# Placing the Sigmoids of the merge gates one product later, and reordering the first ScalarE work of the attention

## The chip, the cores and the metric

The kernel runs on one NeuronCore of a Trainium2 chip. The metric is the time of one execution on the device in microseconds (us), as the median of several runs. One execution is also recorded by the hardware profiler. Engines: TensorE (PE; its weight loads are shown as PEld), VectorE (DVE), ScalarE (ACT), GpSimd (POOL), and SyncE (SP), whose queue issues nearly all DMAs.

## The reference

One decoder layer over x of 2048 rows and 1024 columns (SEQ, D_MODEL), all in float32. A conditioning vector c gives shift, scale and gate. Two token mixers work side by side, a sliding-window attention with sinks and a causal pool over windows of 2, 4, 8 and 16 rows; each has a SiLU gate and an output projection, and two sigmoid gates merge them:

```
mod = silu(c) @ w_ada + b_ada;  shift, scale, gate = split(mod, 3)
u = x * (1 + scale) + shift
q, k, v, a_gate, p_in, p_gate, m_a, m_p = split(u @ w_in)     # widths 1024,128,128,1024,1024,1024,1024,1024
a = (sliding_window_sink_attention(q, k, v, sinks, bias, mask) * silu(a_gate)) @ w_attn_proj
p = ((multiscale_causal_pool(p_in) through w_pool_mix) * pool_scale * silu(p_gate)) @ w_pool_proj
y = (sigmoid(m_a) * a + sigmoid(m_p) * p) @ w_out * (1 + gate)
x = layer_norm(alpha * x + y)
```

There are 16 query heads of 64 columns on 2 key/value heads, and a window and block of 128 rows.

## The kernel before, in words

**Products.** Every large matrix product is done with operands split in two fp32r parts, high and low (three matmuls for one), and with a Strassen-like scheme of seven products on a 2 x 2 blocking instead of eight. One "product" is 12 matmuls of 128 x 128 weights against 512 columns (`product`, L317). The data side of a product is a *set*: B11, T1, T2, B21, T3, B22, T4. Each set lies in SBUF in two halves (blocks 0 and 1, and blocks 2 and 3 of the inner dimension), each half with a high and a low part: ACT casts it to the high part, DVE subtracts to get the low part. The weight side is a `Quad`: four blocks of weights (`W` and `A22`), whose sums POOL makes (`sum1` L269, `mid` L273 and L274, `late` L278), and whose parts ACT (cast, L306 or L313) and DVE (low, L132) write into `w_set` tiles, of which there are four.

**The ring.** Outside the attention, quads go in groups of two. For a group, `front` (L331) makes the opening products with B11 and T1, two for each quad. Then `back` (L341) makes T2 and B21 for the first quad and for the second, T3 and B22 for the first and for the second, and the two T4. That is 14 products for a group with the opening of the next. After each product stands a `tick()`: it first runs the hooks of its position in the group, then everything in the list `due` that `defer(ticks, f)` (L454) put off to this tick. Four accumulators pass to `consume` as they are ready: the first behind B21, then T3, B22 and T4 (the T3 result goes through `p <- lg, p`, L390).

**The order of the queues.** `pe`, `act`, `dve`, `pool` and `sp` are wrappers (`Ordered`, L51). Whatever goes through them is pinned behind the last instruction traced before it on the same engine; their line in the profile is always L57. What is written as `nc.scalar...`, `nc.vector...` is not pinned: the compiler's scheduler places it, by the time at which it expects the operands to be there. Each engine then has one fixed queue.

**Stages.** The head and the first ring compute gates, keys, values and queries of the first half of the rows (1024 rows each); `attention` (L774) follows for the first half; a second ring and `attention` for the second half. Then comes the output part, rings of its own: the merge gates left over, then attention projection, pool projection (first half), attention projection, pool projection (second half), each of two groups, and last the product with w_out with the layer norm. `planned` (L530) hangs the set work of each stage at fixed positions: B11, T1, T2 and B21 and the first half of T3 in the last group of the stage before, the second half of T3, then B22 and T4 by halves at positions 0 to 4 of the stage's first group.

**The merge gates.** Their raw values (`ma_d`, `mp_d`) were stored to DRAM by earlier stages. `gates_ahead` (L599) loads them: at the beginning of `back` two tiles for each quad of the group, and two ticks later the other two, by `sp.dma_start`, and each has its Sigmoid (`nc.scalar.activation`, L607). `consume` of an attention projection (L614) multiplies the result by the gate on DVE (L618); that of a pool projection (L625) multiplies (L627), adds to the attention's part (L629) and stores y.

**The attention.** `attention` writes out by hand, all through the pinned wrappers, the work of 64 blocks of queries (scores, softmax, transposes, values) and, between them, the products of the remaining gates, queries and pool inputs as fill; the list `seq` holds the order of the fill's products, and `split(i)` makes the weights of number i (cast on ACT, low part on POOL or DVE), three products ahead. Numbers 0, 1 and 2 are T2, B21 and T3 of the first quad. At the start (L987 to L997) stand: the load of the last keys and values of the first half (second attention only), the first bias tile, `warm` (an Exp on one column, which makes the table of Exp be loaded), `seed(0)` (ACT copies the first opening accumulator), the copy of the second one to `p5`, and the three first `split`. The two opening products before the attention are made by `front`, with SiLUs of the last gates (L587) about them.

Of the kernel before, what the change touches and what calls it, by code (L numbers as in the profile page):

```python
# [14 lines left out]
AF = mybir.ActivationFunctionType  # L15
# [45 lines left out]
def kernel(  # L61
# [22 lines left out]
    nc = tc.nc  # L84
# [46 lines left out]
    def low(engine, dst, src, hi):  # L131
        engine.tensor_tensor(dst, src, as32(hi), ALU.subtract)  # L132
# [9 lines left out]
    def bank(tag="mm"):  # L142
        return ps.tile([P, CH], F32, tag=tag, bufs={"mm": 4, "lg": 2, "pt": 1, "pv": 1}[tag], name=tag)
# [310 lines left out]
    def defer(ticks, f):  # L454
        due.append((now[0] + ticks, len(due), f))
# [143 lines left out]
    def gates_ahead(name, s, m, raw):  # L599
        g = {}  # L600

        def ahead(ph, turn):
            for mi, t in (((0, 0), (1, 1)), ((0, 1), (1, 0)))[turn]:
                x = g[mi, t] = ph.c("g")
                sp.dma_start(x, gates_d[name][s, m + mi, t])
                if raw:
                    nc.scalar.activation(x, x, AF.Sigmoid)  # L607

        return g, ahead

# [137 lines left out]
    def load_kv(s):  # L748
        if s:
            sp.dma_start(as32(kk[:, :, 0:P]), k_end_d)  # L750
            sp.dma_start(as32(vv[:, 0]), v_end_d)
# [22 lines left out]
    def attention(ph, s, fills, post, opened):  # L774
# [10 lines left out]
        def bias_tile(j):  # L785
            bt = tp.tile([P, 2, 2 * P], F32, tag="bt", bufs=2, name="bt")
            e_src = e_rep[:, 2 * j : 2 * j + 2, :]
            sp.dma_start(bt, bass.AP(e_src.tensor, e_src.offset + P - 1, [[HEADS * ET - 1, P], [ET, 2], [1, 2 * P]]))
            return bt
# [92 lines left out]
        splits = {}  # L882
# [9 lines left out]
        def split(i):  # L892
            x, name = seq[i]
            q = quads[x]
            if name == "B11" and x > 1:
                q.sum1(pool)
            w = ph.split()
            hi, lo = made[i] = w[:, 0:CH], w[:, CH:]
            act.copy(hi, q.block(name))
            low(dve if name == "T1" or (x, name) in on_dve else pool, lo, q.block(name), hi)  # L900
            if name == "T1":
                q.mid(pool)
            elif name == "B21":
                q.late(pool)
# [18 lines left out]
        def seed(x):  # L923
            st[x][2] = bank()
            act.copy(st[x][2], st[x][0])
# [21 lines left out]
        def filling():  # L947
            for i, (x, name) in enumerate(seq):
                begun(i)
                w = made.pop(i)  # L950
                acc = st[x][{"B11": 0, "B21": 0, "T1": 1, "B22": 1}.get(name, 2)]
                for k in range(4):
                    product(acc, w, name, name in ("B11", "T1"), k, k + 1)
                    yield
                ended(i)
# [30 lines left out]
        U = 2 * NB  # L986
        load_kv(s)  # L987
        bts = {0: bias_tile(0)}
        act.activation(warm, mhalf, AF.Exp)
        seed(0)  # L990
        p5 = st[0][3] = tp.tile([P, CH], F32, tag="p5", bufs=2, name="p5")
        act.copy(p5, st[0][1])
        for i in range(-3, 0):
            for j in splits.get(i, ()):
                split(j)
        fill = filling()
        lgs, exps, Ls, pvs, outs, ags = {}, {}, {}, {}, {}, {}  # L997
        total, done = 4 * len(seq), 0
# [1 line left out]
        for n in range(N + 3):  # L1000
            now_n[0] = n
            j, t, b = n // U, n // NB % 2, n % NB
# [547 lines left out]
    with Pools("a0") as ph:  # L1550
        opened = attention(ph, 0, plans[0][1], plans[0][2], opened)
# [4 lines left out]
    with Pools("a1") as ph:  # L1556
        opened = attention(ph, 1, plans[1][1], plans[1][2], opened)
# [3 lines left out]
    with Pools("mix", spare=4, p=2, c=8) as ph:  # L1561
# [10 lines left out]
        for n, (raw, i) in enumerate((raw, i) for raw in (ain_d[1], pin_d[1], wo_d) for i in range(4)):  # L1572
            for offset, f in sums_to(ph, raw, i, load_raw(raw, i)):
                at = int(2 + 8 * n + offset)
                i, gi = every[at // 14]
# [78 lines left out]
```

## Time and profile before

| | us |
|---|---|
| median of 3 runs | 1693.23 |
| lowest, highest | 1687.39, 1694.29 |
| the profiled execution | 1693.3 |
| span of its trace, first to last instruction | 1691.5 |
| PE busy | 1648.7 |
| DVE busy | 1193.7 |
| ACT busy | 1030.0 |
| POOL busy | 988.5 |

The span is what the trace covers; the rest of the execution's time lies around it. Times in rows are microseconds from the first instruction. A row of the timeline has start, duration, engine, line, operation, what it writes and reads, shapes, how many instructions of the kind follow one another, and in brackets how long the engine stood idle before it and what released it. A row of windows has the stretch, its length, PE's busy time with the number of instructions, the granted clock of PE (1.00 is full speed), the DMA share and GB/s.

### The profile page before, as it was taken

The page shows a single profiled execution, that of the slowest core. Times are in us where ns is not written, and L with a number is a line of the kernel's source. Part 1 is how long each engine was busy: PE and PEld are TensorE (multiplying, and loading weights), DVE is VectorE, ACT ScalarE, POOL GpSimd, SP SyncE. Part 2 cuts the span into 40 slices and gives each one's busy share as a digit, 9 for nine tenths or more (in the row PEclk, how much of TensorE's full clock was granted, in tenths as well). Part 3 has the DMA queues.
Part 4 walks back from the last instruction along what each step waited for, and adds up shares of the span by engine and source line. Part 5 has one row for each costly group of instructions (what it writes and reads, how often), then busy time and mean ns, then how long its engine had stood idle before and what let it go on. Part 6 is the DMA issues. An engine that isn't in the chain of part 4 may idle for free.

```text
span 1691.5 us, 24675 instructions
## 1 busy us (share of the span) xinstructions
PE 1648.7 (97%) x8058; PEld 1384.4 (82%) x8058; DVE 1193.7 (71%) x2132; ACT 1030.0 (61%) x2150; POOL 988.5 (58%) x734
## 2 busy tenths in 40 slices
PE   7999999999999999999999999999999999999997
PEld 6788888888888888888788888888878777887886
DVE  6856545676857657357567677676669897989877
ACT  4755457878778755335578777876646445644452
POOL 3343437586857828762476867496567576533442
PEclk9999999999999999999999999999999999999999
DMA  9688843343432478766533344234979797888443
GB/s 359 219 279 307 197 161 102 101 132 108 149 107 99 135 248 308 267 231 211 190 114 99 114 130 156 81 114 135 336 247 363 262 360 259 318 283 271 150 150 112
DMA packets 188849, 336.79 MB, mean 199 GB/s; under 512 B 18336, under 2 KB 44080, under 8 KB 188720
## 3 DMA queue, kind: packets, MB, share of 16 engines
q1 hardware_dynamic: 185600, 330.96, 57.3%
q10 hardware_dynamic: 3088, 4.23, 1.0%
q8 instruction: 64, 1.05, 0.2%
q14 instruction: 65, 0.53, 0.1%
q0 software_dynamic: 32, 0.02, 0.0%
HBM read 227.96 MB, written 110.33 MB: 200 GB/s over the span
## 4 chain that ended last, share of the span: by engine, by line
PE 74%; DVE 8%; DMA 7%; ACT 4%; issue 3%; POOL 3%; SPq 1%; POOLq 0%; DVEq 0%; ACTq 0%
PE mm L57 48%; PE lg L57 19%; PE pv L57 4%; PE pt L57 4%; DVE w_set L132 1%; DMA ain_T<-spare 1%; ACT L L57 1%; DMA g<-ma_d 1%; DMA g<-mp_d 1%; DVE w_set L57 1%; DVE set_T L57 1%; POOL W L269 1%; DMA spare<-pin_B 1%; DVE L L57 1%; ACT w_set L57 1%
## 5 line engine op out<-in xcount | busy, mean ns | idle before, releaser
L57 PE MATMUL mm<-set_B,w_set 128*128 128x512 f32 x2664 | 655.8, 393 | 2.2 <-DVE w_set L132 1.2
L57 PEld LDWEIGHTS mm<-set_B,w_set 128*128 128x128 f32 x2664 | 497.1, 189 | 107.0 <-DVE w_set L132 2.4
L57 PE MATMUL mm<-set_T,w_set 128*128 128x512 f32 x1824 | 455.5, 396 | 5.9 <-DVE mm L57 3.9
L57 PE MATMUL lg<-set_T,w_set 128*128 128x512 f32 x1704 | 412.6, 392 | 10.5 <-DVE p L390 4.4
L57 PEld LDWEIGHTS mm<-set_T,w_set 128*128 128x128 f32 x1824 | 336.7, 189 | 76.2 <-DVE mm L57 6.5
L57 PEld LDWEIGHTS lg<-set_T,w_set 128*128 128x128 f32 x1704 | 319.9, 189 | 81.8 <-ACT w_set L306 5.2
L132 DVE TENSOR_TENSOR w_set<-W,w_set 128x1024 fp32r<-128x1024 f32 x137 | 197.8, 1445 | 142.3 <-ACT w_set L306 129.3
L306 ACT CAST w_set<-W 128x1024 fp32r<-128x1024 f32 x137 | 143.8, 1050 | 212.7 <-PE mm L57 124.3
L57 POOL TENSOR_TENSOR w_set<-W,w_set 128x512 fp32r<-128x512 f32 x120 | 157.3, 1318 | 116.9 <-ACT w_set L57 112.0
L269 POOL TENSOR_TENSOR W<-W,A 128x512 f32<-128x512 f32 x46 | 74.1, 1610 | 232.5 <-DMA A<-in_win_dram 63.5
L57 DVE TENSOR_TENSOR o<-pv,o 64x128 f32<-64x128 f32 x256 | 72.1, 282 | 133.7 <-ACT o L57 127.3
L57 POOL TENSOR_TENSOR spare<-spare 128x512 f32<-128x512 f32 x68 | 124.0, 1826 | 31.5 <-DMA spare<-pin_B 12.2
L57 POOL TENSOR_TENSOR W<-W 128x512 f32<-128x512 f32 x82 | 108.3, 1336 | 53.2 <-DVE sm L57 31.0
L57 ACT ACTIVATE L<-L,nm 128x257 f32<-128x257 f32 (+1 forms) x256 | 127.2, 499 | 9.3 <-DVE nm L57 3.7
L278 POOL TENSOR_TENSOR W<-W 128x512 f32<-128x512 f32 x46 | 72.8, 1583 | 95.9 <-DVE w_set L132 83.5
L57 DVE CUSTOM_DVE_ANT_0 L<-lg,bt,nsink 128x256 f32<-128x256 f32 (+1 forms) x256 | 111.7, 473 | 21.3 <-PE lg L57 11.9
L57 ACT CAST w_set<-W 128x512 fp32r<-128x512 f32 (+1 forms) x165 | 101.4, 628 | 20.9 <-POOL W L57 14.9
L273 POOL TENSOR_TENSOR W<-W 128x512 f32<-128x512 f32 x44 | 72.7, 1656 | 66.3 <-DVE w_set L132 57.2
L57 ACT COPY o<-pv 64x256 f32<-64x256 f32 x128 | 47.4, 370 | 75.9 <-PE pv L57 74.7
L57 DVE TENSOR_TENSOR ptl<-pt,pth 128x512 fp32r<-128x512 f32 (+1 forms) x128 | 85.7, 669 | 1.3 <-ACT pth L57 1.0
L274 POOL TENSOR_TENSOR W<-W 128x512 f32<-128x512 f32 x44 | 71.6, 1628 | 21.9 <-DMA W<-in_win_dram 18.9
L57 ACT ACTIVATE L<-L,sm 128x256 f32<-128x256 f32 (+1 forms) x128 | 64.3, 502 | 31.7 <-DVE sm L57 31.4
(230 smaller groups left out, 2398.2 us busy)
## 6 DMA issues: line engine op xcount, KB each, us to landing
W<-in_win_dram SPq DMA_DIRECT2D x42, 512.0 KB, 5.4
W<-in_win_dram SPq DMA_DIRECT2D x42, 256.0 KB, 3.7
A<-in_win_dram SPq DMA_DIRECT2D x42, 256.0 KB, 4.9
ag_d<-sig SPq DMA_DIRECT2D x32, 256.0 KB, 5.7
pg_d<-sig SPq DMA_DIRECT2D x32, 256.0 KB, 4.4
pg<-pg_d SPq DMA_DIRECT2D x32, 256.0 KB, 3.2
pin_B<-fin SPq DMA_DIRECT2D x32, 256.0 KB, 2.0
ag<-ag_d SPq DMA_DIRECT2D x32, 256.0 KB, 2.9
```

The costliest lines, as they stand in the source:

```text
L57: return lambda *args, **kw: self.tc.keep_in_program_order(op(*args, **kw))
L132: engine.tensor_tensor(dst, src, as32(hi), ALU.subtract)
L269: e.tensor_tensor(self.w[:, 1, :], self.w[:, 2, :], self.a22, ALU.add)
L273: e.tensor_tensor(x[:, 1, :], x[:, 1, :], x[:, 0, :], ALU.subtract)
L274: e.tensor_tensor(x[:, 2, :], x[:, 0, :], x[:, 2, :], ALU.subtract)
L278: e.tensor_tensor(x[:, 3, :], x[:, 3, :], x[:, 1, :], ALU.subtract)
L306: a.copy(by_two(hi), raw)
```

## The change

In `gates_ahead`, each Sigmoid is no longer given out right behind its load but through `defer(1, ...)`: it is traced at the next tick, one product later. At the start of `attention`, the weights of T2 and B21 (`split` of numbers 0 and 1) are made first, then the seed copy, then the warm-up of the Exp table, then the copy to `p5`, and then the weights of T3.

```
@@ gates_ahead
                 sp.dma_start(x, gates_d[name][s, m + mi, t])
                 if raw:
-                    nc.scalar.activation(x, x, AF.Sigmoid)
+                    defer(1, lambda x=x: nc.scalar.activation(x, x, AF.Sigmoid))
@@ attention
         bts = {0: bias_tile(0)}
+        for i in (-3, -2):
+            for j in splits.get(i, ()):
+                split(j)
+        seed(0)
         act.activation(warm, mhalf, AF.Exp)
-        seed(0)
         p5 = st[0][3] = tp.tile([P, CH], F32, tag="p5", bufs=2, name="p5")
         act.copy(p5, st[0][1])
-        for i in range(-3, 0):
-            for j in splits.get(i, ()):
-                split(j)
+        for j in splits.get(-1, ()):
+            split(j)
```

## The prediction

> **What bounds the kernel now.** I read the page, then TensorE's (PE's) busy time in windows, then the order of instructions around each window in which PE lost time. The page first:
>
> ```profile
> span 1691.5 us, 24675 instructions
> ## 1 busy us (share of the span) xinstructions
> PE 1648.7 (97%) x8058; PEld 1384.4 (82%) x8058; DVE 1193.7 (71%) x2132; ACT 1030.0 (61%) x2150; POOL 988.5 (58%) x734
> ```
>
> PE is busy for 97%, so only its idle time (42.8 us, much of it at the head, which the change does not touch) and its slow time (a lowered clock counts as busy) can be won. The windows of the places that the change does touch: the starts of the two attentions, then four first groups and one second group of the stages with the merge gates, 14 products each, cut at starts of products.
>
> ```profile
> 256.10:264.20 8.10, 6.68 (x23) 0.79 0.14 52
> 829.50:836.00 6.50, 5.21 (x23) 1.00 0.42 131
> ```
>
> ```profile
> 1218.20:1263.30 45.10, 41.05 (x168) 0.92 0.78 261
> 1263.30:1301.40 38.10, 38.10 (x169) 1.00 1.03 384
> 1301.40:1343.50 42.10, 39.86 (x169) 0.96 0.70 237
> 1383.80:1423.70 39.90, 39.04 (x169) 1.00 0.70 254
> 1461.90:1500.40 38.50, 38.50 (x169) 1.00 0.60 200
> ```
>
> Columns: length, PE busy (instructions), granted clock, DMA share, GB/s. The group at 1263, a second one, shows no wait: 38.1 us, so 2.72 for a product (12 matmuls). Call the first groups A1 to A4 (starts at 1218, 1301, 1384, 1462; attention, pool, attention, pool): they lose 7.0, 4.0, 1.8 and 0.4 us. Each attention window holds 18 matmuls of fill (18 x 2.72 / 12 = 4.1 us) and one block's scores (0.3 to 0.5 us), so 4.5 us: the first attention loses 3.6, the second 2.0. All of this together is 18.8 us, 1.1% of the time.
>
> **The change part by part. The attention.** Its instructions stand in an order fixed by the program, and each engine works off its queue in order. ScalarE (ACT) around the first start, in two stretches; then PE's waits and GpSimd (POOL):
>
> ```profile
> 247.79 1.28 ACT L57 ACT_TABLE_LOAD   x1
> 249.09 0.20 ACT L57 ACTIVATE warm<-mhalf 128x1 f32<-128x1 f32 x1
> 249.31 1.28 ACT L587 ACT_TABLE_LOAD   x1
> 250.60 1.09 ACT L587 ACTIVATE sig<-lg 128x512 f32<-128x512 f32 x2
> ```
>
> ```profile
> 256.36 0.59 ACT L57 COPY p<-mm 128x512 f32<-128x512 f32 x1 [2.10 <-PE mm L57]
> 256.84 1.66 ACT L57 CAST w_set<-W 128x512 fp32r<-128x512 f32 x3
> 258.40 0.19 ACT L57 COPY L<-nsink 128x2 f32<-128x2 f32 x1
> 258.61 1.28 ACT L57 ACT_TABLE_LOAD   x1
> 259.90 0.40 ACT L57 ACTIVATE L<-L,nm 128x129 f32<-128x129 f32 x1
> ```
>
> ```profile
> 257.51 0.73 PE L57 MATMUL mm<-set_T,w_set 128*128 128x512 f32 x2 [0.80 <-ACT w_set L57]
> 258.87 0.50 PE L57 MATMUL mm<-set_T,w_set 128*128 128x512 f32 x1 [0.62 <-POOL w_set L57]
> ```
>
> ```profile
> 249.77 1.48 POOL L273 TENSOR_TENSOR W<-W 128x512 f32<-128x512 f32 x1
> 257.54 1.28 POOL L57 TENSOR_TENSOR w_set<-W,w_set 128x512 fp32r<-128x512 f32 x1 [6.29 <-ACT w_set L57]
> ```
>
> The warm-up loads Exp's table at 247.79, the last two SiLUs of the gates (L587) load their own over it, and Exp loads its table again at 258.61: it warms nothing. The casts of T2 and B21 stand behind the copy of p5, which waits for the end of the opening products; PE, done with the scores, waits 0.80 us for the cast and 0.62 for POOL's low part. After the change both casts stand ahead of the copies. T2's source is ready when POOL ends L273 at 251.25; the two weight slots are those of the last T4 products, whose results the SiLUs read from 250.60. So the casts fall near 251.3 and 251.9, and POOL, idle for 6.29 us now, makes both low parts (1.28 each) by about 254.5. T3's cast takes a slot that the opening product still reads, and stays behind p5. The warm-up (1.28 + 0.20) fits into the 2.10 us in which ACT waits for p5, behind the SiLUs this time, and the first Exp comes 2.4 us earlier (1.28, and two casts of 1.66 / 3). Late next would be T3's low part, near 259, two products (5.4 us) behind T2's start: not late. I take the whole 3.6 us. Part of it is clock:
>
> ```profile
> 260.50:263.00 2.50, 2.50 (x7) 0.50 0.00 0
> ```
>
> At 0.50, half of 2.50 us is lost: 1.25 us. The Trainium skill (TensorE: Matmul & The Clock Gate, "HAM oscillation — how this bites in real kernels") warns of PE-idle gaps above some 3.4 us; by that rule these short waits would not own the slow clock, it might stay, and the sum would be 1.25 us poorer. The row stands right behind waits of 0.80 and 0.62 us, so here the trace speaks against the rule.
>
> The second attention has one more wait:
>
> ```profile
> 830.36 0.36 PE L57 MATMUL lg<-kk,qs 128*128 128x256 f32 x1 [0.67 <-ACT p L57]
> 832.30 0.50 PE L57 MATMUL mm<-set_T,w_set 128*128 128x512 f32 x1 [0.63 <-POOL w_set L57]
> ```
>
> ```profile
> 825.48 1.09 ACT L587 ACTIVATE sig<-lg 128x512 f32<-128x512 f32 x2
> ```
>
> ```profile
> 827.12 0.32 SPq L57 DMA_DIRECT2D pg_d<-sig  x1
> 827.49 0.53 SPq L57 DMA_DIRECT2D kk<-k_end_d  x1
> ```
>
> ```profile
> DMA to landing us min/median/max: 2.7/2.7/2.7
> ```
>
> The view names p for the scores' wait, but the keys land at 827.49 + 2.7 = 830.2. Their load stands on SP behind the stores of the last SiLUs, which the two table loads (2 x 1.28 + 0.20) hold up. Without these the stores go about 1 us earlier, and so do the keys. Taken: 2.0 us; 1.2 if the keys do not move.
>
> **The Sigmoids.** Nothing is removed or added. The Sigmoids are not pinned to program order: the compiler places them where it expects their data. But a pinned instruction stands behind the last one traced before it on its engine. Given out a product later, the first four Sigmoids of a group are the last on ACT ahead of the cast of B22's first half (A groups), and the next four ahead of T4's first half (A groups) or of B11's second half (second groups). So an A group gains a wait: B22's cast behind the fourth Sigmoid, behind it the low part on VectorE (DVE), behind that PE's B22. On SP the loads keep their order; only a gate stage's store of y and the next weights' load may swap, as equal due times go by the length that the list had, and nothing waits for that store. A1:
>
> ```profile
> 1222.42 1.05 ACT L57 CAST set_B<-set_B 128x1024 fp32r<-128x1024 f32 x1
> ```
>
> ```profile
> 1229.42 3.24 ACT L607 ACTIVATE g<-g 128x512 f32<-128x512 f32 x6
> ```
>
> ```profile
> 1232.00 2.92 PE L57 MATMUL mm<-set_B,w_set 128*128 128x512 f32 x12
> ```
>
> ```profile
> 1233.63 2.34 DVE L57 TENSOR_TENSOR set_T<-set_T 128x1024 fp32r<-128x1024 f32 x2
> ```
>
> ```profile
> 1238.41 2.28 DVE L132 TENSOR_TENSOR w_set<-W,w_set 128x1024 fp32r<-128x1024 f32 x1
> ```
>
> ```profile
> 1240.75 1.65 PE L57 MATMUL lg<-set_T,w_set 128*128 128x512 f32 x3 [4.00 <-DVE w_set L132]
> ```
>
> Now B22's cast stands at 1222.42, 9.6 us ahead of its use at 1232.00. Behind four Sigmoids (3.24 / 6 = 0.54 each) it starts at 1231.6 and its low part ends one to two us behind the cast: up to 2 us late. Against that, A1's long wait is for the third weights' low part at 1238.41, with both lows of T4 (2.34 us) ahead of it on DVE. With T4's first cast behind the Sigmoids, one of these (1.2 us) moves behind, but B22's low moves from a quieter place into the crowd. Ends: 6 us won (the wait and its half clock go, B22 a little late), 1 lost. I take 3.0 won, near the middle, as DVE's work is the same and only its order changes. A3:
>
> ```profile
> 1389.59 2.00 ACT L57 CAST set_B<-set_B 128x1024 fp32r<-128x1024 f32 x2
> ```
>
> ```profile
> 1396.93 1.67 ACT L607 ACTIVATE g<-g 128x512 f32<-128x512 f32 x3
> ```
>
> ```profile
> 1397.45 3.20 PE L57 MATMUL mm<-set_B,w_set 128*128 128x512 f32 x12
> ```
>
> Three Sigmoids end at 1398.6, the fourth 0.54 later, a microsecond less if T4's cast ahead of them goes; so B22's cast ends at 1399 to 1400 against its use at 1397.45: 2 to 3 us late, of which the 1.8 lost now repays a part. Taken 1.5 us lost; ends 0 and 4.5 (with a half clock). A2 and A4, the pool's, have their Sigmoids early:
>
> ```profile
> 1304.11 1.67 ACT L607 ACTIVATE g<-g 128x512 f32<-128x512 f32 x3
> ```
>
> That is one product behind the group's start, B22 being five behind it: taken nothing, ends 2 won and 2 lost together. In second groups B11's cast is due ten products in: nothing.
>
> Sum, against the profiled execution's 1693.3 us (span 1691.5 and 1.8 around it; the runs' median is 1693.23, the same): 1693.3 - 3.6 - 2.0 - 3.0 + 1.5 = **1686.2 us**.
>
> **The rivals.** *The order falls well*: the losses of A1 and A2 go whole and A3 is even: 1693.3 - 5.6 - 11.0 = 1676.7. For it: A1's wait is DVE's order more than its load. Against it: A2 loses 4.0 us although its Sigmoids run early. *The Sigmoids do not move*, so the change does half of what it says: their data come later than the new place, the compiler leaves the order, only the attention pays: 1687.7. For it: none of A1's first six ran before 1229.42. Against it: the pinned cast must go behind four of them. *Slower*: the pinned B22 cast decides. If it costs A2 to A4 what A1 loses now, 7.0 us with the half clock, they pay 3.0, 5.2 and 6.6 more: 1693.3 - 5.6 + 14.8 = 1702.5. It decides from a cast that ends more than some 3 us behind B22's start, as the half clock then follows. Against it: A2's early Sigmoids.
>
> **How the numbers follow.** Forecast 0.47 (its own range 1681 to 1692), good order 0.18, Sigmoids stay 0.25, slower 0.10. The range 1677 to 1701 leaves out half of the good order, most of the slow case and some spill. A measurement here tells about 0.5% (8.5 us) from no change, so faster begins below 1684.8 and slower above 1701.7: faster 0.34 (the good order and a third of the forecast), slower 0.07 (most of the slow case), the rest, 0.59, within.
>
> **What would show it.** Right: Exp's table loaded once at each attention start, the attention windows at about 4.5 us with the clock at 1.00, T2's cast near 251; in A groups B22's first cast behind four Sigmoids, and A1's 4.00 us wait gone or halved. Wrong: an attention window above 5.5 us, a new wait of PE for a B22 set of over 3 us, or over 3 us of change outside all these windows.

## The result, and the profile after

The changed kernel takes 1700.38 us (median of 6 runs, 1698.36 to 1701.77), the kernel before beside it 1690.59 (6 runs, 1687.39 to 1694.29). The ratio is 1.0063, 95% interval [1.0049, 1.0077]: **slower by 0.6%**, where 1686.2 us and a small gain were forecast. The time lies inside the range, the direction is wrong. The medians are 9.8 us apart, the two profiled executions 6.7 (1693.23 and 1699.96): the profile of before is 2.6 us above its median, so the places below add up to 6.7.

The page of after: its span, its busy times, and one group of PE (behind the bar stand busy time, mean ns of one, then the idle time before them and what ended most of it):

```profile
span 1698.2 us, 24675 instructions
PE 1646.6 (97%) x8058; PEld 1385.0 (82%) x8058; DVE 1195.9 (70%) x2132; ACT 1024.8 (60%) x2146; POOL 995.2 (59%) x734
L57 PE MATMUL mm<-set_B,w_set 128*128 128x512 f32 x2664 | 655.8, 393 | 12.9 <-DVE set_B L57 6.9
```

PE is busy for 2.1 us less than before (1648.7) in a span longer by 6.7 us, so 8.8 us of idle time came in. ACT has four instructions less: at each start of the attention one table load is left of three. The group names where PE waits now: for the low part of a B set, 6.9 us.

The windows of after, cut at the same products as those of before: the two attention starts (in the second from the end of PE's last matmul ahead of the scores), then A1, B1, A2, B2, A3, A4, B4:

```profile
257.98:262.52 4.54, 4.54 (x23) 1.00 0.48 168
827.65:833.63 5.98, 4.69 (x23) 1.00 0.57 164
1215.74:1257.71 41.97, 38.85 (x169) 1.00 0.80 278
1257.71:1296.36 38.65, 38.36 (x169) 1.00 1.03 384
1296.36:1336.22 39.86, 38.96 (x169) 1.00 0.73 240
1336.22:1381.81 45.59, 40.30 (x169) 0.96 0.91 337
1381.81:1427.78 45.97, 40.48 (x169) 0.93 0.64 232
1466.36:1504.44 38.08, 38.08 (x169) 1.00 0.51 168
1504.44:1546.76 42.32, 38.45 (x169) 1.00 1.01 357
```

The first attention start is what was forecast: 8.10 us became 4.54 at full clock. The second barely moved. A1 fell from 45.10 to 41.97. But A3 rose from 39.90 to 45.97, and two second groups, of which nothing was expected, rose as well: B2 to 45.59 and B4 to 42.32. Before they were:

```profile
1343.50:1383.80 40.30, 38.64 (x169) 1.00 1.00 364
1500.40:1540.00 39.60, 38.12 (x168) 1.00 0.99 348
```

PE does the same matmuls in the same order in all kernels of this study, so the time from one matmul to a later one can be set side by side. In microseconds, between the starts of the same matmuls; "att 1" and "att 2" are 25 and 20 us about the two starts, so only differences count; single profiles, in which the head (242 to 246 us) differs from run to run by up to 3.8 us with the same instructions:

```
                        att 1  att 2    A1     B1     A2     B2     A3     A4     B4
before                  24.99  19.88  45.09  38.08  42.10  40.33  39.89  38.53  39.60
after                   21.43  19.46  41.96  38.66  39.86  45.59  45.97  38.08  42.31
e1 attention only       21.43  19.65  45.21  38.08  40.05  40.37  39.91  38.08  38.47
e8 its casts only       21.43  19.76  44.36  38.08  38.70  40.32  39.82  38.08  39.63
e9 its warm-up only     23.36  19.85  44.93  38.08  39.90  40.87  39.78  38.61  38.63
e2 Sigmoids only        24.99  19.88  44.17  38.61  42.04  46.33  45.94  38.08  42.30
e3 late, not pinned     21.43  20.21  45.94  38.08  39.38  40.39  39.85  38.08  39.41
e4 own list             21.43  18.66  41.94  38.46  45.36  46.79  45.56  38.11  42.55
e5 the pins alone       24.96  19.88  44.40  38.08  44.22  44.18  45.30  38.34  42.75
e5a pin of B22          23.36  19.89  44.26  38.08  40.02  40.38  48.47  38.08  38.53
e5b pin of B11          24.95  19.89  43.02  38.44  42.97  46.71  38.61  38.93  43.43
e5c pin of T4           23.36  19.85  40.39  38.08  43.87  40.35  44.07  40.32  38.81
e6 keys earlier         21.43  17.93  43.09  38.08  40.71  39.78  39.91  38.76  39.65
e7 e6, T4 later         21.43  17.93  42.04  38.08  42.19  40.35  39.63  39.33  38.92
```

After less before: -3.6 and -0.4 at the attentions, -3.1 in A1, -2.2 in A2, +5.3 in B2, +6.1 in A3, +2.7 in B4, +1.7 in the head, and some tenths elsewhere make the 6.7 us.

**A3, row by row.** ACT in after, then DVE, then PE:

```profile
1387.56 1.04 ACT L57 CAST set_B<-set_B 128x1024 fp32r<-128x1024 f32 x1
...
1392.99 1.05 ACT L57 CAST set_T<-set_T 128x1024 fp32r<-128x1024 f32 x1
1393.95 2.18 ACT L607 ACTIVATE g<-g 128x512 f32<-128x512 f32 x4
1396.04 1.03 ACT L57 CAST set_B<-set_B 128x1024 fp32r<-128x1024 f32 x1
```

```profile
1396.22 1.22 DVE L57 TENSOR_TENSOR set_T<-set_T 128x1024 fp32r<-128x1024 f32 x1
1397.35 1.28 DVE L618 TENSOR_TENSOR wide<-mm,g 128x512 f32<-128x512 f32 x2
1398.55 1.45 DVE L618 TENSOR_TENSOR wide<-p,g 128x512 f32<-128x512 f32 x1
1399.92 2.28 DVE L57 TENSOR_TENSOR set_B<-set_B 128x1024 fp32r<-128x1024 f32 x1
```

```profile
1397.12 1.20 PE L57 MATMUL mm<-set_B,w_set 128*128 128x512 f32 x4 [1.54 <-ACT set_B L57]
1402.25 3.78 PE L57 MATMUL mm<-set_B,w_set 128*128 128x512 f32 x8 [3.94 <-DVE set_B L57]
```

The Sigmoids did not move: 12.1 us behind the group's start (1393.95 - 1381.81), before 13.1 (1396.93 - 1383.8). What moved is the cast of B22's first half, tied behind the fourth of them: from 5.8 us behind the start (1389.59, the first of two) to 14.2 (1396.04). The casts at 1387.56 and 1392.99 are the second halves of B22 and T4 (the loads that they wait for in the trace tell them apart): each is tied to an instruction traced between the two halves, not to the first half, and overtakes it. PE waits 1.54 us for the cast of B22's first half, uses its high part in 4 matmuls, and then waits 3.94 us more, as the low part comes only 2.85 us after the cast's end (1397.07 to 1399.92) and takes 2.28: on DVE a low part of T4 and three gate products (L618) stand ahead of it. Then 8 matmuls take 3.78 us, at half clock.

**B2, row by row.** Here it is the second half of B11, whose cast stood at the group's start (ACT, before, then after), and its low part on DVE (before, then after), and the low part of the weights that opens the next stage:

```profile
1344.30 2.14 ACT L57 CAST set_B<-set_B 128x1024 fp32r<-128x1024 f32 x2
```

```profile
1347.42 1.67 ACT L607 ACTIVATE g<-g 128x512 f32<-128x512 f32 x3
1348.99 1.04 ACT L57 CAST set_B<-set_B 128x1024 fp32r<-128x1024 f32 x1
```

```profile
1353.46 1.22 DVE L57 TENSOR_TENSOR set_B<-set_B 128x1024 fp32r<-128x1024 f32 x1
...
1372.47 1.21 DVE L132 TENSOR_TENSOR w_set<-W,w_set 128x1024 fp32r<-128x1024 f32 x1
```

```profile
1350.63 1.22 DVE L57 TENSOR_TENSOR set_B<-set_B 128x1024 fp32r<-128x1024 f32 x1
...
1364.59 3.46 DVE L629 TENSOR_TENSOR wide<-g,wide 128x512 f32<-128x512 f32 x2
1367.97 1.21 DVE L57 TENSOR_TENSOR set_T<-set_T 128x1024 fp32r<-128x1024 f32 x1
...
1369.71 1.21 DVE L132 TENSOR_TENSOR w_set<-W,w_set 128x1024 fp32r<-128x1024 f32 x1
```

Measured from the group's start (1343.5 and 1336.22), B11's low part goes from 10.0 to 14.4 us, and the opening weights' low part from 29.0 to 33.5. The lows of the next sets follow B11's in DVE's order and slide with it: between the products of the gates (L627, L629), and one of them, of 2.31 us, ahead of the `p <- lg, p` of L390, which it stood behind before. DVE there, before, then after:

```profile
1363.43 0.68 DVE L390 TENSOR_TENSOR p<-lg,p 128x512 f32<-128x512 f32 x1
1364.03 2.30 DVE L57 TENSOR_TENSOR set_T<-set_T 128x1024 fp32r<-128x1024 f32 x1
```

```profile
1359.43 2.31 DVE L57 TENSOR_TENSOR set_T<-set_T 128x1024 fp32r<-128x1024 f32 x1
1361.66 0.68 DVE L390 TENSOR_TENSOR p<-lg,p 128x512 f32<-128x512 f32 x1
```

PE, before and after:

```profile
1373.74 1.20 PE L57 MATMUL mm<-set_B,w_set 128*128 128x512 f32 x4 [1.04 <-DVE w_set L132]
```

```profile
1362.48 3.00 PE L57 MATMUL lg<-set_T,w_set 128*128 128x512 f32 x12 [1.62 <-DVE p L390]
...
1370.97 1.19 PE L57 MATMUL mm<-set_B,w_set 128*128 128x512 f32 x4 [3.67 <-DVE w_set L132]
1372.00 4.28 PE L57 MATMUL mm<-set_T,w_set 128*128 128x512 f32 x11
```

Moving the cast of a set that is due ten products later costs PE 1.62 us and, where a wait of 1.04 was, 3.67, and then half clock (11 matmuls in 4.28 us).

### The profile page after: what moved, and what is told of

Same layout as the page of the kernel before. It is cut to its first block, busy times and chain, and to the rows that moved or that the text cites. A ratio compares the mean times of both kernels' runs of the same rounds, so it can differ in the third digit from the quotient of the medians.

```text
span 1698.2 us, 24675 instructions
## 1 busy us (share of the span) xinstructions
PE 1646.6 (97%) x8058; PEld 1385.0 (82%) x8058; DVE 1195.9 (70%) x2132; ACT 1024.8 (60%) x2146; POOL 995.2 (59%) x734
## 3 DMA queue, kind: packets, MB, share of 16 engines
q8 instruction: 64, 1.05, 0.2%
## 4 chain that ended last, share of the span: by engine, by line
PE 76%; DVE 8%; DMA 7%; ACT 4%; issue 2%; POOL 1%; SPq 1%; POOLq 0%; DVEq 0%; ACTq 0%
PE mm L57 49%; PE lg L57 19%; PE pv L57 4%; PE pt L57 4%; DMA g<-ma_d 1%; DVE set_T L57 1%; DVE w_set L132 1%; ACT L L57 1%; DMA set_T<-ain_T 1%; SPq L57 1%; DVE wide L629 1%; DMA g<-mp_d 1%; DVE g L627 1%; DMA ain_T<-spare 1%; DVE w_set L57 1%
## 5 line engine op out<-in xcount | busy, mean ns | idle before, releaser
L132 DVE TENSOR_TENSOR w_set<-W,w_set 128x1024 fp32r<-128x1024 f32 x137 | 193.5, 1413 | 145.7 <-ACT w_set L306 127.1
L57 POOL TENSOR_TENSOR W<-W 128x512 f32<-128x512 f32 x82 | 108.2, 1333 | 53.1 <-DVE sm L57 32.4
L278 POOL TENSOR_TENSOR W<-W 128x512 f32<-128x512 f32 x46 | 74.7, 1624 | 100.5 <-DVE w_set L132 92.9
L57 ACT CAST w_set<-W 128x512 fp32r<-128x512 f32 (+1 forms) x165 | 101.7, 628 | 25.5 <-POOL W L57 14.1
L273 POOL TENSOR_TENSOR W<-W 128x512 f32<-128x512 f32 x44 | 71.7, 1632 | 69.8 <-DVE w_set L132 60.8
L274 POOL TENSOR_TENSOR W<-W 128x512 f32<-128x512 f32 x44 | 75.3, 1711 | 18.0 <-DMA W<-in_win_dram 14.9
```

Source lines behind the costliest of these rows:

```text
L57: return lambda *args, **kw: self.tc.keep_in_program_order(op(*args, **kw))
L273: e.tensor_tensor(x[:, 1, :], x[:, 1, :], x[:, 0, :], ALU.subtract)
L274: e.tensor_tensor(x[:, 2, :], x[:, 0, :], x[:, 2, :], ALU.subtract)
L278: e.tensor_tensor(x[:, 3, :], x[:, 3, :], x[:, 1, :], ALU.subtract)
```

## The experiments

Theory: the loss is the **pins**. A deferred Sigmoid becomes the last instruction traced on ACT ahead of a pinned cast, which must then follow it; B22's cast holds up A groups, B11's holds up second groups. Each run has its own runs of the kernel before beside it; ratios are to these. Rivals: the attention edit upsets the order further on; the Sigmoids' *lateness* itself; the swapped order of stores and loads on SP.

**The two halves of the change.** e1 has only the hunk in `attention`, e2 only that in `gates_ahead`.

> The change without its Sigmoid part: only the attention's start is reordered, Sigmoids are given out behind their loads as before. Theory (the loss comes from casts of the set B22, pinned behind Sigmoids, and the attention pays): 3.9 us faster than before, 3.5 of it at the first attention, 0.4 at the second; the output stages' windows as before (45.1 us for the group at 1218). Rival 1 (the attention's edit shifts the later rings and costs there): slower than before by 3 us or more.

> The other part alone: Sigmoids one product later, attention as before. Theory: 11 to 14 us slower than before, all of it in the output stages, with PE waiting over 3 us for the B22 set in the third stage's first group. Rival 1 (attention's edit costs): within 3 us of before.

e1: 1687.75 us, ratio 0.9979 [0.9967, 0.9990]. e2: 1703.72, ratio 1.0074 [1.0056, 1.0091]. The attention edit alone is a gain of 0.2%, and B2 and A3 stay at 40.37 and 39.91 us. The Sigmoids alone have the whole loss, in the same groups. The halves add up: 0.9979 x 1.0074 = 1.0053, within the interval of the whole.

**Late, but not pinned.** e3 is the whole change, and behind each pair of deferred Sigmoids stands a copy of one column that waits for nothing. The pinned cast then follows the copy, not the Sigmoid.

```
             if raw:
+                defer(1, lambda: nc.scalar.copy(warm, mhalf))
```

> The whole change, and behind each pair of late Sigmoids a copy of one column on ScalarE, so that the next pinned cast stands behind this copy, which waits for nothing, and no longer behind a Sigmoid. Theory (the pin is what costs): B22's casts go back ahead of the Sigmoids, the waits of 4 us for B22 go, and the time is within 3 us of the run with the attention's part alone, so 1 to 7 us faster than before. Rival 2 (the later Sigmoids themselves, or the swapped order of store and weight load on SP, cost): still 6 us or more slower than before.

1687.67 us, ratio 0.9985 [0.9970, 1.0000]: the loss is gone, with 32 copies more on ACT. ACT in A3 of e3 (start 1381.06):

```profile
1386.80 2.00 ACT L57 CAST set_B<-set_B 128x1024 fp32r<-128x1024 f32 x2
...
1394.15 1.14 ACT L607 ACTIVATE g<-g 128x512 f32<-128x512 f32 x2
```

Both halves of B22 are cast at 5.7 us behind the start again, and the Sigmoids stand at 13.1, where before had them. So giving them out later moves no Sigmoid; without the pin the edit does nothing. Lateness falls as a rival.

**SP's order.** e4 is the whole change with a list of its own for the Sigmoids, so that the stores and loads in `due` keep the order of before. (In the code cuts, `...` stands for lines left out.)

```
+    gate_due = []
...
-                    defer(1, lambda x=x: nc.scalar.activation(x, x, AF.Sigmoid))
+                    gate_due.append((now[0] + 1, lambda x=x: nc.scalar.activation(x, x, AF.Sigmoid)))
```

> The whole change, with the late Sigmoids in a list of their own, so that the numbers in the list of deferred work, and with them the order of y's store and the next weight load on SP, are as before; the pins stay. Theory (pin alone): within 3 us of the change. Rival 2 (the swap on SP makes the new waits of the pool stages' second groups, 5.1 and 2.8 us): 5 to 8 us faster than the change.

1705.88 us, ratio 1.0081 [1.0057, 1.0106]: the loss stays, in B2 (46.79) and A3 (45.56). SP's order is not the cause of it. But e4 was expected within 3 us of the change, and its median is 5.5 us above; the two intervals overlap. In its profile A2 takes 45.36 us, where after takes 39.86; why was not followed up.

**The pins by themselves.** e5 is the kernel before, in which three casts are told to stand behind the Sigmoid traced last: the first halves of B22 and T4 and the second half of B11. No Sigmoid is deferred. e5a, e5b and e5c have one pin each. (Two helper lines shift the line numbers: L611 is L607, L622 is L618.)

```
-            act.copy(t[:, :, 0, :], raw(name, half))
+            pins = sigmoid and (name, half) in (("B22", 0), ("T4", 0), ("B11", 1))
+            with tc.issue_after(sigmoid[0].ins) if pins else ExitStack():
+                act.copy(t[:, :, 0, :], raw(name, half))
...
-                    nc.scalar.activation(x, x, AF.Sigmoid)
+                    sigmoid[:] = [nc.scalar.activation(x, x, AF.Sigmoid)]
```

> The kernel before, its Sigmoids behind their loads and its attention unchanged, with the pins written in: the casts of B22's first half, T4's first half and B11's second half in stages with merge gates may not be issued ahead of the Sigmoid last given out. Theory (the pins cost, not the lateness): 9 to 15 us slower than before, like the Sigmoid part alone. Rival 3 (pins cost only together with later Sigmoids): within 3 us of before.

> Of these pins only that of B22's first half. Theory: the first groups change and the second ones stay: the third stage's first group loses some 6 us more, the first stage's gains about 3; 2 to 7 us slower than before. Rival 4 (one pin shifts the compiler's order everywhere): new waits of 3 us or more in second groups too.

> Of these pins only that of B11's second half. Theory: only second groups change: those ahead of the third and the last stage's openings lose about 5 and 3 us; 4 to 9 us slower than before, the first groups' windows as before. Rival 5 (a cast due ten products in costs nothing, as was predicted; those waits come from B22's and T4's pins upstream): within 2.5 us of before.

> Before, with only the third pin: each cast of T4's first half is tied behind the Sigmoid traced last ahead of it (now the Sigmoids of the same loads, not moved). The pins theory has the loss in the casts of B22 and of B11, whose runs alone cost 1.0048 and 1.006 against 1.0101 of all three; by their difference this one is worth about -0.1%: 0.997 to 1.002, with A1 shorter by 1 to 3 us (T4's low part leaves DVE free for the third weights), A2 and A3 within 1.5 us of before, and no second group changed by over 1 us. The rival, that any pin behind a Sigmoid costs since it holds all pinned work of ACT behind it, has 1.003 or more, with A3 longer by over 3 us.

e5: 1707.63 us, ratio 1.0101 [1.0084, 1.0118]. The pins alone, with nothing deferred, cost at least as much as the Sigmoids' hunk (1.0074). e5a (B22): 1698.95, 1.0048 [1.0030, 1.0067]. e5b (B11): 1700.42, 1.0060 [1.0044, 1.0077]. e5c (T4): 1696.01, 1.0018 [1.0003, 1.0033]. The medians of e5, e5a and e5b are 17.5, 8.8 and 10.2 us above before, each more than its expectation allowed (15, 7 and 9): the sign was right, the sizes were put too low.

The windows of A3 in e5a and of B2 in e5b (e5c's places are in the table):

```profile
1379.16:1427.63 48.47, 41.20 (x170) 0.89 0.64 231
```

```profile
1342.60:1389.31 46.71, 41.05 (x169) 0.93 0.93 341
```

Each pin has its own place: B22's makes A3 8.6 us longer and leaves B2 as it was (40.38), B11's makes B2 longer by 6.4 and B4 by 3.8, and A3 no longer (38.61). So neither needs the other; the rival that one pin upsets the order everywhere falls, as e5a's second groups are as before's or shorter. B22's and B11's are the two that cost most. T4's came out within its expectation as a ratio, but not by its places: it makes A1 shorter by 4.7 us, more than expected, and A3 longer by 4.2 and A2 by 1.8, where 1.5 was the bound. So any of these casts, put behind the Sigmoids, can become the one that is late; the losses differ in size and do not add (0.48 + 0.60 + 0.18% against 1.01).

**The attention's parts.** e8 moves only the casts of T2 and B21 ahead, e9 only the warm-up behind the seed copy.

> Of the attention's part only the two casts ahead of the copies; the warm-up stays where it was. Theory: PE's two waits at the first attention go with the casts, the window from 256 falls by 3 us or more; at the second attention nothing is won, as the last SiLU, and with it the keys, come later still. Rival 8 (the warm-up gives half): the first window falls by 1.5 to 2 us only.

> Of the attention's part only the warm-up, moved behind the seed copy; the casts stay behind the copies. Theory: the first window stays within 0.5 us, since PE waits for casts and not for Exp; the second attention gains the 0.8 us of its scores' wait, as the SiLUs and the keys come a microsecond sooner. Rival 8 (the warm-up gives half): the first window falls by 1.5 to 2 us.

e8: 1689.72 us, 0.9989 [0.9973, 1.0005]. e9: 1689.60, 0.9993 [0.9978, 1.0008]. Neither total can be told from no change. In the traces e8 has all of the first start's gain (21.43 us, as after). e9's first start is 1.63 us shorter than before's, as the rival (the warm-up gives half) had it; the theory allowed 0.5. But e9 keeps both waits of PE (0.80 and 0.62 us), and e5a and e5c, which leave the attention as it was, have the same 23.36 us. So these 1.63 us are not the warm-up's: they are a slow clock that follows the two waits in some profiles and not in others (last section). The casts earn the other 1.93, and leave no wait for the slow clock to follow. At the second start (19.85 us) its scores wait for no keys any more, as the last SiLU's store goes earlier; but PE then waits 0.78 us for T2's cast, where the keys' wait of 0.67 had hidden it.

**The second attention.** Why did it not pay? ACT, SP and PE of after around its start:

```profile
823.64 0.62 ACT L57 CAST w_set<-W 128x512 fp32r<-128x512 f32 x1 [3.01 <-POOL W L273]
824.17 0.59 ACT L587 ACTIVATE sig<-lg 128x512 f32<-128x512 f32 x1
```

```profile
823.92 2.33 SPq L57 DMA_DIRECT2D pg_d<-sig  x2
826.31 0.53 SPq L57 DMA_DIRECT2D kk<-k_end_d  x1
```

```profile
828.98 0.71 PE L57 MATMUL lg<-kk,qs 128*128 128x256 f32 x4 [1.29 <-ACT L L57]
```

T2's cast stands ahead of the last SiLU now and waits 3.01 us for POOL. The SiLU waits behind it, its store behind the SiLU, the keys' load behind the store on SP, and the scores behind the keys, 2.7 us from the issue at 826.31, as before. (The view names ACT, long done; in e1 the same wait, 1.47 us there, is put down to the keys' DMA.) The wait for the cast went, the wait for the keys grew. e6 is e1 with the keys' load hung at an earlier position of the second ring:

```
-        load_kv(s)
...
+        hooks.setdefault((4, 6), []).append(lambda: load_kv(1))
```

> The attention's part alone, and the load of the last keys and values for the second attention given out eight products earlier, ahead of the last stores of the gates. Theory (that wait is for the keys, behind the stores): PE's wait of 1.6 us at the second attention's scores goes, and the time is 1 to 2 us below the attention's part alone, 5 to 6 us below before. Rival 6 (the wait is for ScalarE, as the view names it): the wait stays at 1.3 us or more.

```profile
826.53 0.64 PE L57 MATMUL lg<-kk,qs 128*128 128x256 f32 x4
```

The scores of e6 wait for nothing, and the second start takes 17.93 us, 1.95 less than before: the 2.0 us that the prediction had claimed. The total, 1687.95 us, 0.9981 [0.9970, 0.9991], cannot be told from e1's, and the 5 to 6 us below before that were expected did not come: it is 2 to 3. The 1.7 us against e1 are 0.1%, less than the intervals resolve.

**A1's queue on DVE.** In A1 the third weights' low part waits behind both low parts of T4. e7 is e6 with T4's two halves hung two positions later.

```
-    SPLIT_AT = (2, 3, 4, 5, 6, 7, 11, 12, 13, 14, 15, 16, 17, 18)
+    SPLIT_AT = (2, 3, 4, 5, 6, 7, 11, 12, 13, 14, 15, 16, 19, 20)
```

> The run with the keys earlier, and the cast and low part of T4 in the first groups given out two products later (positions 5 and 6 of the group; T4 is used at 8). Theory (the first groups' own waits are DVE's order: T4's lows stand ahead of the third weights' low part): the 4 us wait in the first stage's first group goes, its window falls from 43 to 45 us to 40 or less, and the time is 3 to 6 us below the run with the keys earlier. Rival 7 (DVE has too much work there whatever the order): the window stays within 1.5 us, or as much is lost at T4.

1683.89 us, ratio 0.9951 [0.9932, 0.9969]: **faster than both kernels**, than before by 0.5%. But the reason is confirmed only in part. A1 takes 42.04 us, where 40 or less was expected; that is 1.05 less than in e6, within the 1.5 of the rival (DVE has too much work there whatever the order). PE still waits for the third weights:

```profile
1233.77 1.19 PE L57 MATMUL lg<-set_T,w_set 128*128 128x512 f32 x4 [1.83 <-DVE w_set L132]
```

The profiled execution of e7 is not shorter than that of e6 (1686.2 and 1685.0 us): e7's is 2.3 us above its median and e6's 2.9 below. So where the rest of the difference of medians lies, these profiles do not show.

## Why the prediction was wrong

- **Failed: "In second groups B11's cast is due ten products in: nothing."** It looked at when the moved instruction's own result is due. What counted was the queue: the cast of its second half went from 1.9 to 12.8 us behind the group's start, its low part moved by 4.4 us, and with it the order of DVE's work behind it, down to weights that came 1.04 us late already. B2 and B4 together lost 8.0 us; e5b, that pin alone, shows it.
- **Mis-sized: "Taken 1.5 us lost" for A3; it was 6.1, beyond the end of 4.5 too.** The mechanism was right: B22's cast goes behind four Sigmoids, and PE waits for B22. The cast was late by less than expected (ended at 1397.07, PE waiting 1.54 us). The step that failed is "its low part ends one to two us behind the cast", said of A1 and carried over to A3: it ended 5.1 us behind (1397.07 to 1402.20), as DVE's queue stood between. e5a alone loses even 8.6 there.
- **Wrong: "Taken: 2.0 us; 1.2 if the keys do not move" at the second start; it was 0.4.** The keys did move, but the wrong way: measured from the product ahead of them on PE, their load goes out 0.8 us later than before, as the SiLU behind the moved cast set when. The prediction counted two table loads less on ACT ahead of the store, and not the 3.0 us for which T2's cast itself waits for POOL. That wait was in its own text on the first start ("T2's source is ready when POOL ends L273"); it was not asked who stands behind. e6 gets the 2.0.
- **Right: the first start, 3.6 us**, and by the casts, as worked out (e8). But 1.6 of the 3.6 are slow clock, and that before's profile had it was luck: e9, e5a and e5c have the waits without it. The prediction held that two short waits owned the slow clock; e5a and e9 go against that as a rule, with the same two waits and no slow clock behind (below). The Trainium skill (TensorE: Matmul & The Clock Gate, "HAM oscillation — how this bites in real kernels") warns of gaps above some 3.4 us. Before's row has the slow clock behind waits of 0.80 and 0.62 us all the same.
- **A1, 3.0 us won: 3.1 were measured, by the trade described, but the size is in part luck.** Its 4.00 us wait for the third weights is gone, and B22 waits instead, 3.01 us where up to 2 were expected. PE ran on at full clock behind that wait. In e5 the same wait of 3.01 us is followed by the half clock, and A1 takes 44.40; in e2, the Sigmoids' hunk alone, it takes 44.17. With the order of before (e1, e3, e6, e8, e9) it takes 43.1 to 45.9. Of e5a to e5c only T4's pin is clearly below that (40.39).
- **Right: A4 nothing, SP's swap harmless** (e4). A2 and A4 together won 2.7 us, a little over the two allowed, but A2's 2.2 are no gain of the change: kernels with the order of before in this group (e1, e8, e9) have 38.7 to 40.1 us there as well, and 1.6 of before's 42.1 are the half clock behind a wait of 2.24 us (below).
- **The rival "the pinned B22 cast decides", 1702.5 us at a chance of 0.10**, was near in time. It had the half clock behind a late B22, seen in A3. But it put the loss into A2 to A4; two of these three lost nothing, and the second groups, which no rival named, lost 8.0 of the 14.1 us lost in B2, A3 and B4.
- **"The Sigmoids do not move" was true** (12.1 and 13.1 us), and still not its 1687.7: the rival took a Sigmoid that stays for a change that does nothing.
- **The signs of being wrong** that the prediction named all came: an attention window of 5.98 us, a new wait of 3.94 us for B22, and over 3 us (B2) outside the windows it listed.

## What to carry to other kernels

Where pinned and free instructions share a queue, ask of a moved free instruction not where it will run, but which pinned instruction is traced next behind it on its engine: the pin binds that one. An operand that is due ten products later is no cover if the rest of its making stands in an in-order queue ahead of work that is due sooner. Before an instruction is put earlier in a queue, look at what it waits for itself: that wait is handed to all behind it.

## What the hardware showed that was not expected

**The slow clock does not follow from the length of a wait.** At the first attention start, before had waits of 0.80 and 0.62 us and then a clock of 0.50. PE of e9, at the same place:

```profile
258.50 0.73 PE L57 MATMUL mm<-set_T,w_set 128*128 128x512 f32 x2 [0.80 <-ACT w_set L57]
259.86 2.56 PE L57 MATMUL mm<-set_T,w_set 128*128 128x512 f32 x10 [0.62 <-POOL w_set L57]
```

The same waits, and 10 matmuls in 2.56 us, at full speed, where before took 3.97 (e5a and e5c have the same 23.36 us there). Of the seven profiles with both waits, before, e2, e5 and e5b have the slow clock behind them, e5a, e5c and e9 not. Nor is it the longer waits alone. PE of before in A2, and of after and of e5 in A1, at the same matmul:

```profile
1328.30 4.48 PE L57 MATMUL lg<-set_T,w_set 128*128 128x512 f32 x12 [2.24 <-DVE p L390]
```

```profile
1233.59 2.12 PE L57 MATMUL mm<-set_B,w_set 128*128 128x512 f32 x8 [3.01 <-DVE set_B L57]
```

```profile
1237.39 3.78 PE L57 MATMUL mm<-set_B,w_set 128*128 128x512 f32 x8 [3.01 <-DVE set_B L57]
```

2.24 us idle, and the next product takes 4.48 instead of 2.88. 3.01 us idle, and the next 8 matmuls run at full speed in after and at half speed in e5. In the output groups of all fourteen profiles, every wait of 3.16 us and above was followed by the slow clock, as in B2 and A3 of after; the shorter ones by either, down to one of 1.77 us (e2, A2). The Trainium skill (TensorE: Matmul & The Clock Gate, "What's actually happening") says that the clock is set over a free-running window of some 3.4 us; the long waits agree with this, and a dependence on where a wait falls would fit the mixed short ones. No run here varied the phase by itself, so that stays open. For a forecast it means, as an estimate from 3.78 against 2.12 and 4.48 against 2.88 us, some 1.6 us of chance for each shorter wait; single profiles that differ by that much in a group prove nothing.

**An operation of DVE takes up to twice as long beside POOL.** In A3 of after, T4's low part at 1396.22 took 1.22 us, while POOL was idle, and B22's at 1399.92, of the same shape, 2.28, with POOL at work all along:

```profile
1398.17 1.27 POOL L269 TENSOR_TENSOR W<-W,A 128x512 f32<-128x512 f32 x1 [7.47 <-DVE wide L618]
1399.41 1.71 POOL L57 TENSOR_TENSOR spare<-spare 128x512 f32<-128x512 f32 x1
1401.08 2.25 POOL L274 TENSOR_TENSOR W<-W 128x512 f32<-128x512 f32 x1
```

POOL's own operations grew as well: those of this shape take 1.29 us where no operation of DVE lies beside them (the median of 58 in this trace), and up to 2.25 here. The ends alternate: POOL at 1401.12, DVE's low part at 1402.20, POOL at 1403.33. Each ends 1.1 us behind the other, a little less than the 1.22 and 1.29 us that it takes alone, as if it had stood still until the other was done, with the wait counted as busy time. The Trainium skill (SBUF — State Buffer, "SBUF: two separate sides") has a VectorE operation with two SBUF inputs and a GpSimd one that reads SBUF share a pair of ports under an exclusive lock. The alternating ends agree with that, though no run here tests it by itself. So a low part that slides into a busier stretch becomes longer besides being late: 1.1 us of A3's loss.
